# Three small changes to the planner that orders a transformer block's instructions: VectorE may wait a moment, one chain is priced as dependent, one reciprocal goes before a product group

## The chip, the cores and the metric

The kernel runs on one core of one Trainium2 chip. The metric is the device time of one execution in microseconds (us). The engines are TensorE (PE; its weight loads are PEld), VectorE (DVE), ScalarE (ACT), GpSimd (POOL) and SyncE (SP, which issues nearly all DMAs here). They run apart from each other and meet at semaphores. Each executes its own instructions strictly in the order in which the program lists them.

## The reference

One block of a streaming encoder on x of 512 tokens by 1024 channels, float32:

```python
x = x + 0.5 * swiglu_ffn(rms_norm(x), w13, w2)          # first feed-forward half step, 2816 hidden
h = rms_norm(x)
a, g, q, k, v, f = split(h @ w_in)                      # 512 each, f: 8 heads
y_conv = conv_module(a, g)    # a*sigmoid(g), causal depthwise conv of 31 taps, LayerNorm, silu
# forgetting attention, 8 heads of 64, causal:
D = cumsum(log_sigmoid(f + b_f))
y_attn = softmax(q @ k.T / 8 + D[t] - D[s]) @ v
x = x + concat(rms_norm(y_conv), rms_norm(y_attn)) @ w_out
x = x + 0.5 * swiglu_ffn(rms_norm(x), w13b, w2b)        # second half step
out = rms_norm(x)
```

## The kernel before

Channels lie on the 128 partitions, the 512 tokens along the free axis; x is held on chip as eight tiles of 128x512. Weights stream from HBM in units of 128x1024 or so (`raw`). To keep float32's accuracy at the faster matmul format, each weight and each activation is split in two: ScalarE rounds it to a high part (`whi`, `xh`), VectorE subtracts to get the low part (`wlo`, `xl`), and a product is three matmuls: high by high, high by low, low by high. The feed-forward down products (tiles `f1p`, `f2p`) are arranged in seven instead of eight sub-products per block pair, which needs sums and differences of weights on VectorE and GpSimd.

The stages in order of time: first feed-forward part (`f1...`); then, in the middle, the mixer: the gated inputs of four convolution tiles (`pg`, `pa`), values and gate logits (`pv`, `zf`), and for four pairs of heads i the products `pq`, `pk`, the scores `s`, their transposes `pt` and the weighted sum `po`; then the output projection (`wo`); then the second feed-forward part (`f2...`) and the final norm with the stores.

Nearly all matmuls belong to a stream of products whose order is fixed (`ORDER = "c0 c1 c2 v c3 a0 a1 n a2 a3 w0 w1 w2 w3"` in the middle). The convolution's 31 taps are a chain of multiply-adds for each tile: tiles 1 and 3 on VectorE (`conv<-u,par,conv`, accumulated in PSUM), tiles 0 and 2 on ScalarE (multiply, `tap`) and GpSimd (add, `acc<-acc,tap`). `conv_norm` normalises the four tiles when all are done.

The forget gates: `values()` makes `zf` in eight small steps, then the log-sigmoid as one joined chain of 16 VectorE instructions on 128x32 tiles (`e`, `lf`). Joined instructions are one step of the plan and are issued together. `gates()` transposes `lf` (`pc`, behind the product `pq` of the first pair of heads), makes the cumulative sums with one scan (`cum`), writes them to DRAM on SP's queue, from where each head's row is loaded, spread over all partitions (`ck`). The step that adds `ck` to the scores and takes the row minimum is `sm<-s,ck` with `mn`.

The order of every engine's instructions is not written by hand: the block first records all steps in a `Plan`, and `schedule` then puts them in order. Each step has a cost from `price` (a formula per engine and operation) and a rank: the longest path of costs from it to the end, plus its own urgency, a number that the code gives some steps (`URGENT_V`, `URGENT_LF`, `URGENT_LN`, `URGENT_STATS` 200; the attention 80; the `x` updates in the feed-forward part 50; q and k 3; weights' splits and taps none). The scheduler walks through a modelled time: for each engine it picks, among the steps whose inputs all have a place already, the one that can start first, and among equals the one of the highest rank; of the engines' picks the earliest is put in the order. A step that depends on another of the same engine may start 0.03 us behind its end on VectorE (`SAME`), while the engine counts as free 0.08 us before that end (`OVERLAP`). The price of a step that joins several instructions is the sum of theirs.

The end of the kernel: the last down products are made in parts: tokens 0 to 255, then 256 to 383 and 384 to 511. For each part `scales` sums the squares (`ssq_out`), takes the square root on ScalarE and the reciprocal on VectorE (`rc_out`), spreads it by two matmuls (`rb_out`), and `finish` multiplies three groups of tiles by it on VectorE and stores each (`out_d`), from SP's queue, but for one group of the last part from ScalarE's.

All instructions are emitted in one place, so the profile puts them all at line 248; tiles' names tell them apart.

## Time and profile before

| | before |
|---|---|
| median of 3 runs | 943.43 us (942.79 to 943.44) |
| the profiled execution | 943.39 us |
| its span, first to last instruction | 941.7 us |
| mean granted TensorE clock | 0.998 of full speed |
| PE busy | 930.4 us (99%), 5277 matmuls |
| DVE busy | 654.4 us (69%), 990 instructions |
| ACT busy | 431.3 us (46%), 676 instructions |
| POOL busy | 155.1 us (16%), 132 instructions |
| HBM read, written | 88.21 MB, 2.11 MB |

Rows of the timeline give the start in us from the span's start, the length in us, engine, line, operation, output <- inputs, form and count; in brackets the idle time of the engine just before and what ended it. Where several instructions of a kind stand in a row, they are merged and the length is that of all. Rows of waits give the total, the number of times and the longest. Rows by stretches give the stretch, its length and the busy time of PE, PEld, DVE, ACT and POOL with the counts of instructions, then the granted clock, the DMA share and GB/s. The lengths of matmuls overlap, since they are pipelined: they start some 0.227 us apart at 128x512.

### The profile page before, as it was taken

How to read it: one execution, taken by the hardware profiler on the slowest of the kernel's cores; microseconds unless marked ns; L12 is line 12 of the kernel's file. 1: busy time of each engine (PE TensorE's matmuls, PEld its weight loads, DVE VectorE, ACT ScalarE, POOL GpSimd, SP SyncE). 2: the span in 40 equal slices, each digit the busy share in tenths (PEclk: the TensorE clock that was granted, in tenths of full speed). 3: DMA queues.
4: the chain of work that ended last, by engine and by line, in shares of the span. 5: the costliest groups of instructions: out<-in, count | busy, mean ns of one | idle time of the engine just before them, and what ended most of it. 6: DMA issues, size and time to landing. Idle time of an engine off the chain costs nothing.

```text
span 941.7 us, 13473 instructions
## 1 busy us (share of the span) xinstructions
PE 930.4 (99%) x5277; PEld 794.2 (84%) x5277; DVE 654.4 (69%) x990; ACT 431.3 (46%) x676; POOL 155.1 (16%) x132
## 2 busy tenths in 40 slices
PE   9999999999999999999999999999999999999997
PEld 7888999988999888897776777888899988999887
DVE  6655887756876475799987776555777755876554
ACT  6433433334333245666878655333433333433344
POOL 1000211001112000889763000000111001111000
PEclk9999999999999999999999999999999999999999
DMA  7222323132333132223221112223332222332222
GB/s 248 91 90 93 131 90 112 69 109 71 134 113 106 52 97 104 91 93 109 90 69 49 64 68 90 90 90 98 122 116 90 90 90 90 123 101 96 67 84 90
DMA packets 34207, 91.19 MB, mean 97 GB/s; under 512 B 3544, under 2 KB 13912, under 8 KB 34144
## 3 DMA queue, kind: packets, MB, share of 16 engines
q1 hardware_dynamic: 33600, 90.13, 28.3%
q8 instruction: 41, 0.67, 0.3%
q10 hardware_dynamic: 544, 0.20, 0.1%
q14 instruction: 22, 0.18, 0.1%
HBM read 88.21 MB, written 2.11 MB: 96 GB/s over the span
## 4 chain that ended last, share of the span: by engine, by line
PE 92%; DVE 4%; ACT 2%; issue 1%; DMA 1%; SPq 0%; DVEq 0%
PE f2g L248 13%; PE f2u L248 13%; PE f1u L248 13%; PE f1g L248 13%; PE f2p L248 9%; PE f1p L248 9%; PE wo L248 5%; PE f1o L248 3%; PE f2o L248 3%; PE s L248 2%; PE pg L248 2%; PE pa L248 2%; DVE conv L248 2%; PE pq L248 1%; PE pv L248 1%; PE pk L248 1%
## 5 line engine op out<-in xcount | busy, mean ns | idle before, releaser
L248 ACT CAST whi<-raw 128x1024 fp32r<-128x1024 f32 (+3 forms) x152 | 150.8, 992 | 266.1 <-issue 84.5
L248 DVE TENSOR_TENSOR wlo<-raw,whi 128x1024 fp32r<-128x1024 f32 (+3 forms) x152 | 185.6, 1222 | 17.5 <-ACT whi L248 17.0
L248 POOL TENSOR_TENSOR acc<-acc,tap 128x512 f32<-128x512 f32 x60 | 90.9, 1516 | 82.9 <-ACT tap L248 78.4
L248 PE MATMUL f1u<-xh,whi 128*128 128x512 f32 x176 | 68.9, 391 | 0.4 <-ACT xh L248 0.4
L248 PE MATMUL f1u<-xl,whi 128*128 128x512 f32 x176 | 68.6, 390 | 0.3 <-DVE xl L248 0.3
L248 PE MATMUL f2g<-xh,whi 128*128 128x512 f32 x176 | 68.7, 390 | 0.0
L248 PE MATMUL f2g<-xl,whi 128*128 128x512 f32 x176 | 68.6, 390 | 0.0
L248 PE MATMUL f2u<-xh,whi 128*128 128x512 f32 x176 | 68.6, 390 | 0.0
L248 PE MATMUL f1u<-xh,wlo 128*128 128x512 f32 x176 | 68.5, 389 | 0.0
L248 PE MATMUL f2u<-xl,whi 128*128 128x512 f32 x176 | 68.5, 389 | 0.0
L248 PE MATMUL f2u<-xh,wlo 128*128 128x512 f32 x176 | 68.5, 389 | 0.0
L248 PE MATMUL f2g<-xh,wlo 128*128 128x512 f32 x176 | 68.5, 389 | 0.0
L248 PE MATMUL f1g<-xh,whi 128*128 128x512 f32 x168 | 65.8, 392 | 0.0
L248 PE MATMUL f1g<-xl,whi 128*128 128x512 f32 x168 | 65.7, 391 | 0.0
L248 PE MATMUL f1g<-xh,wlo 128*128 128x512 f32 x168 | 65.6, 390 | 0.0
L248 POOL TENSOR_TENSOR f2S<-raw 128x512 f32<-128x512 f32 x8 | 11.3, 1408 | 311.7 <-DMA raw<-w2b 227.8
L248 DVE TENSOR_TENSOR f2un<-f2u,rstd_f2in 128x512 f32<-128x512 f32 x22 | 15.2, 691 | 63.4 <-PE f2u L248 63.4
L248 POOL TENSOR_TENSOR f1S<-raw 128x512 f32<-128x512 f32 x8 | 10.4, 1295 | 261.7 <-DMA raw<-w2a 194.4
L248 DVE TENSOR_TENSOR f1un<-f1u,rstd_in 128x512 f32<-128x512 f32 x22 | 15.2, 690 | 54.5 <-PE f1u L248 54.5
L248 ACT ACTIVATE tap<-u,par 128x512 f32<-128x512 f32 x60 | 42.3, 720 | 16.0 <-POOL acc L248 15.8
L248 DVE SCALAR_TENSOR_TENSOR conv<-u,par,conv 128x512 f32<-128x512 f32 x60 | 45.1, 752 | 1.2
L248 PEld LDWEIGHTS f1u<-xh,whi 128*128 128x128 f32 x176 | 33.2, 188 | 7.8 <-ACT xh L248 0.8
(420 smaller groups left out, 2408.1 us busy)
## 6 DMA issues: line engine op xcount, KB each, us to landing
raw<-w13b SPq DMA_DIRECT2D x44, 512.0 KB, 3.5
raw<-w13a SPq DMA_DIRECT2D x42, 512.0 KB, 3.4
raw<-w2a SPq DMA_DIRECT2D x16, 512.0 KB, 3.6
raw<-w2b SPq DMA_DIRECT2D x16, 512.0 KB, 3.6
raw<-wag SPq DMA_DIRECT2D x8, 512.0 KB, 3.5
raw<-wqk SPq DMA_DIRECT2D x8, 512.0 KB, 3.5
raw<-wo SPq DMA_DIRECT2D x8, 512.0 KB, 3.4
raw<-w2a SPq DMA_DIRECT2D x16, 192.0 KB, 2.4
```

Of the source, the lines that this page charges most:

```text
L248: ins = getattr(target, method)(*real, **kw)
```

## The change

- In `schedule`, once VectorE's pick is known, a loop looks at its other ready steps. One that can start later than the pick, but by less than 0.4 us and 0.6 of the pick's own cost (`AHEAD`), and whose rank is more than 80 above the pick's (`MORE`), takes the pick's place: VectorE then waits for it.
- In `values`, the joined log-sigmoid chain is priced 16 x 0.035 = 0.56 us higher.
- In `scales` of the very last part, the last product of the group before (tokens 256 to 383, tiles 6 and 7), which `finish` has noted in `waiting`, is made dependent on the new reciprocal, so that it cannot be put ahead of it.
- The load of `x` at the start gets a branch for `k < 0` and a condition `k >= 0`; k runs from 0 to 7.

```diff
+AHEAD, MORE = 0.4, 80.0
...
                 pick = None
+                soon = []
                 for op in ready[e]:
...
                     key = (t, -rank, op.index)
+                    soon.append((op, t))
                     if pick is None or key < pick[0]:
                         pick = (key, t, op)
+                if pick and e == "V":
+
+                    until = pick[1] + min(AHEAD, 0.6 * pick[2].cost)
+                    for op, t in soon:
+                        if pick[1] < t < until and op.rank - MORE > -pick[0][1]:
+                            pick = ((t, -op.rank, op.index), t, op)
...
                 V.reciprocal(c, c)
+                if ts.stop == T:
+
+                    waiting[0].before[id(plan.ops[-1])] = plan.ops[-1]
                 r = bank(*banks[1])[:, :n * P]
...
                     V.tensor_mul(xt, xt, r.over(b - a))
+                    waiting[:] = [plan.ops[-1]]
...
-        behind, summed = [], []
+        behind, summed, waiting = [], [], []
...
+        if k < 0:
+            with plan.urgent(7000.0 - 100 * k):
+                S.dma_start(out=xs[k], in_=x_d[:, k, :])
         with plan.urgent(4950.0 - 100 * k):
-            Q.dma_start(out=xs[k], in_=x_d[:, k, :])
+            if k >= 0:
+                Q.dma_start(out=xs[k], in_=x_d[:, k, :])
...
-        plan.join("V")
+        chain = plan.join("V")
+
+        chain.cost += 16 * 0.035
```

## The prediction

> **What bounds the kernel.** I read the page first, then the list of what TensorE waited for, then busy time by stretches, and last the instruction order of single engines round each wait that was left.

> ```profile
> span 941.7 us, 13473 instructions
> PE 930.4 (99%) x5277; PEld 794.2 (84%) x5277; DVE 654.4 (69%) x990; ACT 431.3 (46%) x676; POOL 155.1 (16%) x132
> ```

> ```profile
> PE s L248 <- DVE k L248: 1.5, 1, 1.5
> PE pt L248 <- ACT pT L248: 1.5, 1, 1.5
> PE warm L248 <- POOL eps L248: 1.1, 1, 1.1
> PE rb_out L248 <- DVE rc_out L248: 1.0, 1, 1.0
> PE s L248 <- DVE mn L248: 0.5, 1, 0.5
> ```

> The page says that TensorE is busy 99% of the span. A change that only puts VectorE's instructions (DVE) in another order takes nothing from TensorE's 930.4 us; it can shorten only the 941.7 - 930.4 = 11.3 us in which TensorE stands still. The waits say where these are: one at the start (`warm`, untouched), three in the middle (1.5 for `k`, 1.5 for `pT`, 0.5 for `mn`: 3.5 us), one at the end (`rc_out`); the rest is the last update and store behind the last product.

> ```profile
> 421.00:435.00 14.00, 14.00 (x64) 11.59 (x63) 13.27 (x29) 9.08 (x15) 12.04 (x10) 1.00 0.23 75
> 435.00:450.00 15.00, 13.04 (x64) 10.02 (x63) 14.76 (x25) 8.63 (x16) 12.68 (x7) 1.00 0.40 141
> 511.00:530.00 19.00, 17.50 (x153) 13.62 (x153) 16.22 (x28) 15.80 (x31) 5.67 (x7) 1.00 0.11 40
> 530.00:925.00 395.00, 395.00 (x2201) 339.47 (x2200) 261.58 (x382) 157.73 (x230) 21.76 (x16) 1.00 0.27 93
> ```

> The columns are length, then busy time of PE, PEld, DVE, ACT and POOL. VectorE's mean of 69% hides a stretch where it is the tight engine: 13.27 of 14 us and 14.76 of 15 us from 421 to 450, and it is there that TensorE loses 1.96 us. Behind 530 it has 133 us to spare while TensorE never stops.

> **Part 1: the gates' steps cost 0.56 more in the plan.** No instruction is added; the plan's clock of VectorE moves. The joined chain has 16 instructions. By `price`, those that touch PSUM cost 0.15 + 32 x 0.00105 = 0.18 (six), 0.15 + 32 x 0.00118 = 0.19 (nine `scalar_tensor_tensor`), and the reciprocal 0.35: 3.14 us. On the chip:

> ```profile
> 421.18 0.18 DVE L248 SCALAR_TENSOR_TENSOR e<-zf 128x32 f32<-128x32 f32 x1
> 421.29 1.22 DVE L248 TENSOR_TENSOR wlo<-raw,whi 128x1024 fp32r<-128x1024 f32 x1
> 422.42 0.19 DVE L248 TENSOR_SCALAR e<-e 128x32 f32<-128x32 f32 x1
> 425.96 0.19 DVE L248 SCALAR_TENSOR_TENSOR lf<-e,e 128x32 f32<-128x32 f32 x1
> ```

> From 422.42 to 425.96 + 0.19 = 426.15 are 3.73 us, and 3.14 + 0.56 = 3.70. So the plan believed VectorE to be 0.56 us further on than it was, and now it does not. The chain's own result isn't urgent: `gates` uses `lf` only behind the product of `pq`, at 435. What the correction moves is the choice among the instructions that follow:

> ```profile
> 435.83 0.38 PE L248 MATMUL pc<-ident,lf 128*8 128x128 f32 x2
> 441.28 0.39 PE L248 MATMUL pk<-xh,wlo 128*128 128x512 f32 x1
> 444.54 0.46 PE L248 MATMUL s<-k,q 128*128 128x128 f32 x2 [1.51 <-DVE k L248]
> 436.32 1.55 DVE L248 SCALAR_TENSOR_TENSOR conv<-u,par,conv 128x512 f32<-128x512 f32 x2
> 437.78 0.68 DVE L248 SCALAR_TENSOR_TENSOR q<-pq,rstd_f1n 64x512 f32<-64x512 f32 x1
> 438.38 1.20 DVE L248 TENSOR_TENSOR_SCAN cum<-one,pc 8x512 f32<-8x512 f32 x1
> 441.39 0.69 DVE L248 SCALAR_TENSOR_TENSOR q<-pq,rstd_f1n 64x512 f32<-64x512 f32 x1
> 442.12 1.55 DVE L248 SCALAR_TENSOR_TENSOR conv<-u,par,conv 128x512 f32<-128x512 f32 x2
> 443.70 0.69 DVE L248 TENSOR_TENSOR k<-pk,rstd_f1n 128x512 f32<-128x512 f32 x1
> 444.96 2.06 DVE L248 TENSOR_TENSOR wlo<-raw,whi 128x1024 fp32r<-128x1024 f32 x1
> ```

> The product `pk` ends at 441.28 + 0.39 = 441.67, yet `k` starts at 443.70, behind two convolution taps that were issued when `k` could already run: the wait of 1.51 us. In the plan a tap may start only 0.03 behind the tap before it and another instruction 0.08 before that tap's end, so a ready `k` always wins over a tap. Two taps ahead of it mean that in the plan `k` came ready only after the second tap was due. A plan that is 0.56 later here sees it ready one tap sooner, unless the overhang was more than 0.56 of a tap's pitch of 1.55 / 2 = 0.78, which leaves some 0.56 / 0.78, 7 in 10 by my estimate. **Term: -0.78 us**, `k` one tap earlier. Bounds: -1.51 (both taps go) and +1.29, if instead the `wlo` that now stands behind `k` comes ahead of it in the place of one tap (2.06 + 0.78 - 1.55, an estimate from these rows). I take the middle reading because it needs no other instruction to change place. Late next, behind `k`, is that `wlo`, and behind it `mn`, whose wait of 0.5 us I leave as it is.

> [...]

> **Part 2: VectorE waits for far more urgent work.** In `schedule` the new loop looks at instructions that are in `ready`, whose inputs all have a place in the order already, so it can wait only for a result that is being made, and at most 0.4 us. A rank is the longest path to the end plus the step's own urgency. The attention's steps (urgency 80) are not 80 above a tap of the last convolution tile: the tap's own path, through the rest of its taps, the normalisation and the first half of the output product, is longer. `k` and `q` have urgency 3. So it can touch the eight `zf` steps and the scan (urgency 200), the sums of squares (200), and in the two feed-forward parts splits against the updates of `x`, which are due a whole group of columns later. Behind 530 the row above gives the cover: 133 us of VectorE against waits of 0.4. Between 396 and 440 it costs at most 9 x 0.4 = 3.6 us of VectorE, and what queues behind are the taps. They have a cover too:

> ```profile
> 477.10 0.75 DVE L248 SCALAR_TENSOR_TENSOR conv<-u,par,conv 128x512 f32<-128x512 f32 x1
> 481.38 3.34 POOL L248 TENSOR_TENSOR acc<-acc,tap 128x512 f32<-128x512 f32 x2 [0.97 <-ACT tap L248]
> ```

> The normalisation needs all four tiles, and GpSimd's ends at 484.72, 6.9 us behind VectorE's last tap at 477.85. Without that cover 3.6 us would go straight onto the normalisation and from there to `wo`. If the scan passes `q`, the cumulative sums leave up to 0.60 us earlier (438.38 - 437.78), their DMA to DRAM and the two loads of `ck` on SP's queue with them, ahead of no weight load that TensorE waits for; `q` is 1.2 later and still long before `k`. **Term: 0**, bounds -0.5 (the wait for `mn` goes) and +0.8 (a tap's pitch lost ahead of `k`).

> **Part 3: the last reciprocal ahead of a product group.**

> ```profile
> 935.54 0.26 ACT L248 ACTIVATE rc_out<-ssq_out,eps 128x1 f32<-128x1 f32 x1
> 935.85 0.41 DVE L248 TENSOR_TENSOR x<-x,rb_out 128x256 f32<-128x256 f32 x1
> 936.19 0.15 DVE L248 RECIPROCAL rc_out<-rc_out 128x1 f32<-128x1 f32 x1
> 936.49 0.46 PE L248 MATMUL rb_out<-ident,rc_out 128*128 128x128 f32 x2 [0.98 <-DVE rc_out L248]
> 936.98 1.35 DVE L248 TENSOR_TENSOR x<-x,rb_out 128x256 f32<-128x256 f32 x3 [0.64 <-PE rb_out L248]
> 936.51 0.47 SPq L248 DMA_DIRECT2D out_d<-x  x1
> 937.43 0.37 SPq L248 DMA_DIRECT2D out_d<-x  x1
> ```

> The square root ends at 935.80, the third product of the group before stands from 935.85, and the reciprocal starts at 936.19. With the new order it starts where that product started, about 935.86: 0.33 us earlier, and the chain broadcast, last products, last store follows without another partner. The passed product then runs from about 935.97 to 936.38, inside the wait for the broadcast (936.98 - 0.33 = 936.65). Its store moves from 936.51 to some 936.6 and occupies SP's queue until 937.07; the next one is due at 937.43 - 0.33 = 937.10: just free. **Term: -0.33**, bounds 0 and -0.41 (the whole product).

> The moved `x` loads add nothing: `k < 0` never holds in a loop from 0, and the other condition always does.

> **Sum.** -0.78 + 0 - 0.33 = -1.11 us. The profiled execution took 943.39 us (span 941.7), the median of the runs is 943.43, which is the same. 943.39 - 1.11 = 942.3 us.

> **The rivals.**
> - *Only the tail moves.* `k` keeps its two taps, as the plan's error at this point may be larger than 0.56: the plan put `q`, whose product ends before the transposes `pc` at 435.83, at 437.78. Time 943.39 - 0.33 = 943.1. The scan's late place speaks for it; that 0.56 is most of a tap speaks against.
> - *Faster: the middle waits close.* With `k` at once and `mn` no longer late it is 1.51 + 0.5 + 0.33 = 2.34 us: 941.1. The `pT` wait is ScalarE's:

> ```profile
> 507.43 1.52 ACT L248 ACTIVATE acc<-acc,par 128x512 f32<-128x512 f32 x2
> 511.50 1.32 ACT L248 ACTIVATE yh<-acc,par 128x512 fp32r<-128x512 f32 x2
> 512.73 0.45 ACT L248 COPY pT<-pt 128x384 f32<-128x384 f32 x1
> ```

>   The copy stands behind the whole row of normalisation steps from 507.43; if the shifted plan puts it some steps forward, 1.5 more goes, 939.6 in all. It needs luck, since no part aims at it.
> - *Slower: a doubled split ahead of `k`.* One mechanism: the later plan finds a weight's split due before `k`, and on the chip it collides with GpSimd:

> ```profile
> 433.25 2.31 DVE L248 TENSOR_TENSOR wlo<-raw,whi 128x1024 fp32r<-128x1024 f32 x1
> 432.66 5.42 POOL L248 TENSOR_TENSOR acc<-acc,tap 128x512 f32<-128x512 f32 x3
> ```

>   This split took 2.31 us beside the accumulations, against 1.22 for the same one at 421.29. Put ahead of `k` with both taps still there it gives 943.39 - 0.33 + 2.31 = 945.4. It decides from 2.2 us of new wait on. For it: the stretch is full, and the `wlo` at 444.96 stands right behind `k`. Against: it would have to jump only one place, yet keep both taps ahead. [...]
> - *Small loss inside the noise band:* the waits of part 2 are spent in vain and a tap's pitch reaches TensorE once or twice: 943.39 - 0.33 + 0.78 to + 1.56, 943.8 to 944.6.

> **How the numbers follow.** Forecast 0.36 (its own range 941.5 to 943.0), only the tail 0.20, small loss 0.08, faster 0.22, slower 0.14. 0.2% is 1.89 us, about what a measurement of this kernel can tell from no change: below 941.5 is faster, above 945.3 slower. So faster 0.22, same 0.36 + 0.20 + 0.08 = 0.64, slower 0.14. The range runs from 940.6, half of the faster case's second step, to 945.3, where the slower case begins; about 0.05 lies below it and 0.14 above.

> **What would show it.** In the profile after: TensorE's busy time within 1 us of 930.4; the wait of `s` for `k` near 0.7 instead of 1.5, with one tap between the second `q` and `k`; the last reciprocal right behind the square root and ahead of a product of 128x256, the wait for `rc_out` near 0.65; no wait of TensorE beyond 530 before the tail. Wrong I would be if a wait for `wlo` or a second wait for `pT` appears between 421 and 530, or if the waits there vanish altogether: the plan is greedy, and a small shift of its clock can change any choice behind 422.

## The result: slower by 2.8 us, and the profile after

| | before | after |
|---|---|---|
| median | 943.22 us (7 runs, 942.57 to 943.59) | 946.02 us (7 runs, 944.72 to 947.26) |
| ratio, with its 95% interval | | 1.003 (1.002 to 1.004) |
| the profiled execution, its span | 943.39, 941.7 us | 946.79, 945.0 us |
| mean granted TensorE clock in it | 0.998 | 0.996 |

The forecast was 942.3 us in a range of 940.6 to 945.3. The changed kernel lies above it. All its instructions stand at line 249 instead of 248. The page's first lines, then what TensorE waited for (total, times, longest, in us):

```profile
span 945.0 us, 13474 instructions
PE 933.1 (99%) x5277; PEld 795.6 (84%) x5277; DVE 656.9 (70%) x990; ACT 432.6 (46%) x677; POOL 153.9 (16%) x132
```

```profile
PE pa L249 <- DVE wlo L249: 2.8, 1, 2.8
PE warm L249 <- POOL eps L249: 1.1, 1, 1.1
PE rb_out L249 <- DVE rc_out L249: 0.7, 1, 0.7
PE wo L249 <- DVE yl L249: 0.6, 1, 0.6
PE f1p L249 <- DVE x L249: 0.5, 1, 0.5
PE f2p L249 <- DVE x L249: 0.4, 1, 0.4
```

Two things changed at once. TensorE is busy 2.7 us longer with the same 5277 matmuls. And the waits for `k` (1.5), `pT` (1.5) and `mn` (0.5) are gone, but a single one of 2.8 us for a weight's split stands where before there was none, in the last convolution tile's product `pa`; behind it come 0.6 for `yl` and, in the two feed-forward parts, 0.5 and 0.4 for updates of `x`. VectorE's timeline round the new wait (start, length):

```profile
421.66 0.19 DVE L249 SCALAR_TENSOR_TENSOR e<-zf 128x32 f32<-128x32 f32 x1
421.76 0.75 DVE L249 SCALAR_TENSOR_TENSOR conv<-u,par,conv 128x512 f32<-128x512 f32 x1
422.42 0.19 DVE L249 TENSOR_SCALAR e<-e 128x32 f32<-128x32 f32 x1
...
425.96 0.19 DVE L249 SCALAR_TENSOR_TENSOR lf<-e,e 128x32 f32<-128x32 f32 x1
426.07 2.24 DVE L249 TENSOR_TENSOR wlo<-raw,whi 128x1024 fp32r<-128x1024 f32 x1
428.23 0.68 DVE L249 TENSOR_TENSOR gn<-pg,rstd_f1n 128x512 f32<-128x512 f32 x1
```

Before, the same split stood at 421.29, ahead of the log-sigmoid chain, and took 1.22 us. Now the chain (422.42 to 426.15, 3.73 us as before) stands ahead of it, and the split runs beside GpSimd's accumulations and takes 2.24. In the traces of before and after a split of 128x1024 that begins while GpSimd runs no TENSOR_TENSOR takes 1.19 to 1.23 us. One that begins beside a running one takes longer by about the time that is left of it, but for one (at 439.51 before, 1.19 us beside an accumulation of 3.69); an accumulation that begins beside a running split is longer too. So here: before, the split began first, and the accumulation that began at 421.87 took 1.78 us instead of 1.3; after, an accumulation runs from 425.96 to 427.23, 1.16 us beyond the split's start, and the split takes 1.02 us more. The split ends at 428.31; TensorE had been ready since 425.56:

```profile
425.17 0.39 PE L249 MATMUL pa<-xl,whi 128*128 128x512 f32 x1
428.37 0.50 PE L249 MATMUL pa<-xh,wlo 128*128 128x512 f32 x1 [2.81 <-DVE wlo L249]
428.70 0.39 PE L249 MATMUL pa<-xh,whi 128*128 128x512 f32 x1
...
430.46 0.63 PE L249 MATMUL pa<-xh,whi 128*128 128x512 f32 x1
430.89 0.63 PE L249 MATMUL pa<-xl,whi 128*128 128x512 f32 x1
...
435.10 0.39 PE L249 MATMUL pq<-xh,whi 128*128 128x512 f32 x1
```

The wait isn't all. From 429.6 on the same matmuls start 0.43 us apart instead of 0.227, until 433. The 22 matmuls left of `pa` take 435.10 - 428.37 = 6.73 us, where 22 x 0.227 are 4.99: 1.74 us more, and that is most of TensorE's longer busy time. By stretches (length, busy time of PE, PEld, DVE, ACT, POOL, then the granted clock) the clock is seen to be halved:

```profile
425.00:428.00 3.00, 0.56 (x3) 0.13 (x1) 2.83 (x7) 1.93 (x3) 2.84 (x3) 1.00 0.00 0
429.00:430.00 1.00, 1.00 (x5) 0.81 (x4) 1.00 (x2) 1.00 (x2) 0.46 (x1) 0.82 0.71 143
430.00:433.00 3.00, 3.00 (x8) 2.32 (x7) 2.89 (x5) 1.52 (x3) 2.66 (x2) 0.50 0.72 243
433.00:434.00 1.00, 1.00 (x6) 0.80 (x5) 0.96 (x2) 0.00 (x0) 0.21 (x1) 0.97 0.44 176
435.00:450.00 15.00, 15.00 (x73) 12.22 (x72) 14.14 (x18) 9.24 (x13) 12.35 (x9) 1.00 0.31 107
```

With the first matmul of some tiles as marks, the span's 3.4 us more come from here:

| from the first matmul of | to that of | before | after | difference |
|---|---|---|---|---|
| start | `f1p` | 106.8 | 106.3 | -0.5 |
| `f1p` | `pg` (tile 0) | 254.9 | 255.6 | +0.8 |
| `pg` | `pq` (pair 0) | 68.4 | 73.2 | +4.7 |
| `pq` | `wo` | 80.0 | 77.4 | -2.5 |
| `wo` | `f2g` | 66.3 | 66.8 | +0.5 |
| `f2g` | first `rb_out` | 351.8 | 352.4 | +0.6 |
| first `rb_out` | end | 13.4 | 13.3 | -0.2 |

The first row differs from execution to execution (105.9 to 108.0 in the 13 profiles of this study). The stages behind it hardly do: where two kernels have the same order in a stage, the clock is the same and no update of `x` is passed over, its length agrees within 0.04 us, with two exceptions (0.34 and 0.14). So the marks show differences that the medians can't. The 0.8 and the 0.6 are the stages with the waits for updates of `x`.

The 4.7 are, but for 0.2, the wait of 2.8 and the slow clock of 1.74. The -2.5 behind it are the old waits for `k`, `mn` and most of that for `pT`: with TensorE 4.7 us later, VectorE and ScalarE are no longer late there. That is why the row 435 to 450 now shows TensorE busy for all of its 15.00 us.

**Why the plan did this.** In the changed plan's own clock, VectorE's pick at 418.02 us was the split (rank 452). The joined log-sigmoid chain, rank 593, could start 0.07 us later. That is inside the 0.4 us and more than 80 above, so VectorE waited 0.07 us and took up a step of 3.70 us. The rule looks at how soon the urgent step can start, not at how long it runs, nor at when the passed step is due.

### The profile page after: what moved, and what is told of

Read it like the earlier page. It is cut to its first block, busy times and chain, and to the rows that moved or that the text cites. A ratio compares the mean times of both kernels' runs of the same rounds, so it can differ in the third digit from the quotient of the medians.

```text
span 945.0 us, 13474 instructions
## 1 busy us (share of the span) xinstructions
PE 933.1 (99%) x5277; PEld 795.6 (84%) x5277; DVE 656.9 (70%) x990; ACT 432.6 (46%) x677; POOL 153.9 (16%) x132
## 4 chain that ended last, share of the span: by engine, by line
PE 91%; DVE 4%; ACT 2%; DMA 1%; issue 1%; SPq 0%; DVEq 0%; ACTq 0%
PE f2g L249 13%; PE f2u L249 13%; PE f1u L249 13%; PE f1g L249 13%; PE f2p L249 8%; PE f1p L249 8%; PE wo L249 4%; PE f1o L249 3%; PE f2o L249 3%; PE pa L249 2%; PE pq L249 2%; PE s L249 2%; PE pk L249 2%; PE pg L249 2%; PE pv L249 1%; DVE conv L249 1%
## 5 line engine op out<-in xcount | busy, mean ns | idle before, releaser
L249 POOL TENSOR_TENSOR acc<-acc,tap 128x512 f32<-128x512 f32 x60 | 88.1, 1468 | 86.9 <-ACT tap L249 82.4
L249 PEld LDWEIGHTS f1u<-xl,whi 128*128 128x128 f32 x176 | 33.0, 188 | 7.9 <-DVE xl L249 1.1
```

The source lines that it names most:

```text
L249: ins = getattr(target, method)(*real, **kw)
```

## Experiments

Each was run in turn with the kernel before; the medians of before in the three groups of runs (a, b, c) are 943.35, 943.37 and 943.36 us. Changes in order were made behind the plan where one place was meant, so that everything else stays as it was.

**One split back ahead of the chain.** The changed kernel's order, with only that one instruction moved:

```diff
         order = self.schedule()
+        order.remove(self.split)                          # wlo of tile 3's pa
+        order.insert(order.index(self.chain), self.split) # ahead of the log-sigmoid
...
```

> The order of the changed kernel with one instruction moved: the split wlo for the product pa of convolution tile 3 is issued in front of the log-sigmoid chain instead of behind it. All else stays in the changed kernel's order. Theory 1 (this one place is the loss): TensorE's wait for wlo of 2.8 us goes, and with it the 1.7 us that the slow clock behind it cost (22 matmuls in 6.73 us instead of 22 x 0.227 = 4.99), so about 946.8 - 4.5 = 942.2 us in the profiled execution, 0.1% below the kernel before. Theory 2 (the reordering as a whole costs, many small delays): at most half of it goes, 944.5 us or more. Under theory 1 the clock stays at 1.00 from 421 to 440.

Measured 944.52 us (943.73 to 945.38, 11 runs), ratio 1.0014 (1.0005 to 1.0023). The wait of `pa` is gone and the clock is 1.00 throughout 421 to 435; in its place some of the old waits come back:

```profile
PE s L249 <- DVE k L249: 1.3, 1, 1.3
PE rb_out L249 <- DVE rc_out L249: 0.7, 1, 0.7
PE wo L249 <- DVE yl L249: 0.6, 1, 0.6
PE pk L249 <- DVE wlo L249: 0.6, 1, 0.6
PE f1p L249 <- DVE x L249: 0.4, 1, 0.4
```

One instruction's place carries 1.5 of the 2.8 us. The other 1.2 or so remain. So theory 1 was right in its signs (no wait, full clock) and wrong in its time, since it counted none of the waits that come back.

**The same split moved behind the chain in the kernel before.**

```diff
         order = self.schedule()
+        order.remove(self.split)
+        order.insert(order.index(self.chain) + 1, self.split)
...
```

> The mirror image: the order of the kernel before with the same one split moved from in front of the log-sigmoid chain to right behind it, nothing else. Theory 1: TensorE waits for this split at pa, some 1.5 us (chain from 421.9 to 425.5, split to 426.7, needed at 425.2) up to 2.6 us if GpSimd doubles it; VectorE's total work is unchanged, so the later wait for k (1.5 us) shrinks by about as much, and the time is 943.2 to 944.9 us, the upper end if the clock falls behind the wait. Theory 2: the place of the split is harmless, 943.2 us with no wait for wlo.

Measured 945.0 us (944.37 to 945.46), ratio 1.0016 (1.0007 to 1.0025): this single move costs 1.65 us. The chain starts earlier here than in the changed kernel (421.29, not 422.42) and the split takes 1.48 us, not 2.24 (GpSimd's accumulation ends 0.40 us behind its start), so the wait is shorter:

```profile
PE pa L248 <- DVE wlo L248: 1.7, 1, 1.7
PE pt L248 <- ACT pT L248: 1.5, 1, 1.5
PE s L248 <- DVE k L248: 1.1, 1, 1.1
```

The granted clock stays at 1.00 behind this wait of 1.7.

**The reciprocal alone** (the changed kernel with rule and price switched off, so that only the dependence in `scales` is left beside the kernel before; one pair of VectorE's instructions changes places).

```diff
...
+                if ts.stop == T:
+                    waiting[0].before[id(plan.ops[-1])] = plan.ops[-1]
```

> The kernel before with the reciprocal's edge alone: on every engine the order differs from the kernel before by one swap, the last reciprocal ahead of one product. Prediction: 0.33 us less, the wait for rc_out 0.65 instead of 1.0. Rival: something else ends last (the stores), 0.0.

Measured 943.24 us, ratio 0.9997 (0.9988 to 1.0006). The wait for `rc_out` is 0.7 instead of 1.0, and from the first `rb_out` the last one comes 0.33 us earlier (7.93 us instead of 8.26). The end comes only 0.16 us earlier (13.27 instead of 13.44), because the last store takes longer from issue to landing: 2.30 us instead of 2.15. In the 13 profiles this goes with its distance to the store two ahead of it: 2.30 to 2.34 where that is 1.06 to 1.09 us (eight profiles), 2.13 to 2.17 where it is 1.37 to 1.40 (five). In the median what the step is worth is less than these runs can tell from nothing.

**Without the rule** (the chain's price and the reciprocal stay).

```diff
-                if pick and e == "V":
+                if False and pick and e == "V":
```

> The changed kernel without the waiting rule: the dearer chain and the reciprocal's edge remain. The prediction's mechanism by itself: k behind one tap instead of two, wait for k 0.7 us, 942.3 us. Rival: the shifted plan makes another wait in the mixer and the time is 943.0 us or more; if it is about 946, the chain's price and not the rule is to blame.

Measured 943.62 us (942.59 to 944.72), ratio 1.0002 (0.9993 to 1.001). The profiled execution took 942.64 (span 940.9). Its waits:

```profile
PE wo L249 <- DVE yl L249: 1.0, 1, 1.0
PE rb_out L249 <- DVE rc_out L249: 0.7, 1, 0.7
PE wo L249 <- ACT yh L249: 0.6, 1, 0.6
PE s L249 <- DVE k L249: 0.6, 1, 0.6
```

The rule's whole loss is gone. The price did what the forecast said, one tap instead of two between the second `q` and `k`, a wait of 0.6 where 0.7 was forecast, and the wait for `mn` is gone too. But in place of the 1.5 us for `pT` stand 1.6 us at `wo` for the normalised convolution outputs, and in the median the gain isn't seen. In the profile it is: from `pq` to `f2g` this kernel takes 0.65 us less than before (145.58 instead of 146.23), and with the tail's 0.17 it is 0.83 us shorter from `f1p` to the end. Its three runs at a mean clock of 0.998 took 942.64 to 942.81 us, its four at 0.996 943.55 to 944.01, and the four at 0.997 942.59 to 944.72.

A second finding comes from the plan alone: with the rule on, the chain's price changes nothing. The changed kernel without the 0.56 has the same order on all five engines.

**The wait filled with idle matmuls.** The changed kernel, with 11 more matmuls inside the 2.8 us, overwritten by the product itself:

```diff
...
+            if k == 0:
+                for m in range(fill):          # 11 for pa of tile 3, else 0
+                    PE.matmul(ps, hi[:, k], ah[k], start=True, stop=True)
+                step.cost = 0.0
```

> The changed kernel with eleven idle matmuls (11 x 0.227 = 2.5 us) in front of the first matmul of the product pa that waits for the late split. Each starts its sum anew, so they leave nothing in the result. They fit into the wait of 2.8 us: if that wait alone costs, nothing changes (946.0 us) and the wait shows as 0.3 us behind the idle matmuls. Theory A (TensorE's standstill brings the slow clock, which costs up to 1.7 us more): with TensorE kept busy the clock stays at 1.00 behind it, the median falls by 0.8 to 1.7 us to 944.3 to 945.2, and the spread of the runs (2.5 us before) narrows to about 1 us. Theory B (the slow clock has another cause, the loads that run at that time or chance): clock near 0.5 for some us as before, 946 us.

Measured 946.16 us (944.85 to 948.11, 6 runs), ratio 1.0029 (1.0017 to 1.0041). In the profile the clock is 1.00 from 425 to 435 and `pg` to `pq` takes 71.6 us instead of 73.2, which is the 1.6 us of slow clock; but the median didn't fall. This profile has waits elsewhere that the other lacks or has smaller, `xh` at the start 1.1 and `f2p` 1.0: by the marks the start took 0.9 us longer, the stage with `f2p` 0.6 and the tail 0.1, so that the span is the same 945.0. So the run settled the clock in one profile and not the time.

**The split ahead, and no update of `x` passed over.** The rule also lets VectorE leave updates of `x` in the feed-forward parts; here it may not, and the split is moved as in the first experiment:

```diff
-                if pick and e == "V":
+                if pick and e == "V" and pick[2].urgent != URGENT_X:
...
```

> The changed order with the split in front of the chain (as in the first run of this study) and with the waiting rule not applied where VectorE's pick is an update of x in the feed-forward parts. TensorE's, ScalarE's, GpSimd's and SP's orders are the same as there; only VectorE's order in the two feed-forward parts returns to that of the kernel before. If the rule costs there, the waits of f1p and f2p for x (0.4 and 0.2 us) go and the time falls from 944.5 to 943.9 us. Rival: these waits are covered by later slack, 944.5 us as before.

Measured 943.66 us (943.05 to 944.36), ratio 1.0003 (0.9994 to 1.0012). The waits of `f1p` and `f2p` are gone, and 0.86 us against the first experiment with them. With both harms of the rule out, what is left is no difference from before that can be measured.

**`k` first, in the kernel before.** The two taps ahead of `k` are put behind it:

```diff
+        at = order.index(self.k0)
+        taps = [o for o in order[:at] if o.engine == "V"][-2:]
...
+        order[at + 1:at + 1] = taps
...
```

> The kernel before with the two convolution taps that stand ahead of k put behind it, nothing else. The prediction's reading of that wait (k is late by its taps, and TensorE gains what k gains) gives 1.5 us less, 941.8 us, with no wait of s for k. Rival, formed after the run without the rule: what is late next takes the gain. s runs 1.5 us earlier, but the scores' next step needs ck from DRAM and stands behind the 2.06 us split, so the wait for mn grows from 0.5 to about 2 us and the time stays at 943.3 us.

Measured 944.44 us (942.86 to 945.25), ratio 1.0006 (0.9997 to 1.0015). The wait for `k` is gone, and what was late next takes the gain: the wait for `mn` is 2.0 us, where before it was 0.5.

```profile
PE s L248 <- DVE mn L248: 2.0, 1, 2.0
PE pt L248 <- ACT pT L248: 1.5, 1, 1.5
```

Its runs fall in two groups: five at a mean granted clock of 0.998 took 942.86 to 943.81, and six at 0.996 or 0.997 took 944.44 to 945.25. The kernel before has no run at 0.996 in 88.

**A rule for short steps only**, that passes over no update of `x`; price and reciprocal as in the changed kernel:

```diff
-                if pick and e == "V":
+                if pick and e == "V" and pick[2].urgent != URGENT_X:
...
-                        if pick[1] < t < until and op.rank - MORE > -pick[0][1]:
+                        if pick[1] < t < until and op.cost < 2.0 and op.rank - MORE > -pick[0][1]:
```

> The changed kernel with the rule limited: VectorE may wait only for steps that cost under 2 us (so not for the log-sigmoid chain), and not in the place of an update of x. The plan is made anew, so the mixer's order differs in many places. If the two harms named are all, it is no slower than the run without the rule: 943.6 us or less, no wait for wlo and none of f1p or f2p. Rival: any new order of the mixer brings waits of its own, 944 to 945 us.

Measured 942.39 us (941.98 to 943.58, 11 runs), ratio 0.999 (0.9981 to 0.9998): the best of all kernels here, 1.0 us below before and 3.6 below the changed one. Price and reciprocal are in it too. By the marks it is 0.92 us shorter than before from `f1p` to the end, where the kernel without the rule is 0.83 shorter: by the two profiles, both at a mean clock of 0.998, the rule for short steps adds 0.1 us. The medians of the two are 1.2 us apart; no run here has a mean clock of 0.996, and four there have, but that this is all of it isn't shown.

**The long wait left in, without and with filling.** The last question was what the wait and the clock are worth apart. First the changed kernel with no update of `x` passed over, the split left behind the chain:

> The changed kernel, with the rule kept from passing over updates of x; the order of VectorE differs in 28 rows, the split of `wlo` stays behind the log-sigmoid chain. Theory A (the two harms add, and the wait of 2.8 us for `wlo` also slows TensorE's clock for some 3.5 us in part of the runs): wait of `pa` for `wlo` 2.8, waits of `f1p` and `f2p` for x gone, 946.0 - 0.9 = 945.1, runs spread over some 2 us with a lower mean clock (0.996) in the longer ones. Theory B (the clock has nothing to do with the spread): same median, runs within 1 us of each other.

Measured 945.54 us (943.62 to 947.64, 11 runs), ratio 1.0021 (1.0012 to 1.003). Three of its runs have a mean clock of 0.998 (943.62 to 945.12), the other eight 0.995 to 0.997 (945.2 to 947.64). The profiled execution, the longest, shows the slow clock twice as long as in the changed kernel:

```profile
427.00:428.00 1.00, 0.00 (x0) 0.00 (x0) 1.00 (x1) 0.81 (x1) 0.92 (x2) 0.98 0.00 0
428.00:429.00 1.00, 0.40 (x1) 0.40 (x2) 1.00 (x2) 0.00 (x0) 1.00 (x1) 0.50 0.00 0
430.00:433.00 3.00, 3.00 (x8) 2.32 (x7) 2.93 (x4) 1.76 (x3) 2.42 (x2) 0.50 0.72 235
434.00:435.00 1.00, 1.00 (x5) 0.77 (x3) 0.76 (x1) 0.00 (x0) 0.11 (x1) 0.61 0.00 0
435.00:440.00 5.00, 5.00 (x23) 4.13 (x22) 3.08 (x4) 2.77 (x4) 3.30 (x3) 1.00 0.00 0
```

Then the same with the 11 matmuls of the filling; no other row of any engine differs:

> As the kernel without the passed updates of x, with 11 matmuls more ahead of the waiting product of `pa`, which are overwritten by the product itself, so that TensorE isn't idle in the wait. Theory A: no run at a mean clock of 0.996, no slow stretch behind the wait, and a median some 0.7 us lower than without the filling (1.7 us in the share of runs that had the slow clock, about 4 in 10). Theory B: the same median within 0.3 us.

Measured 944.22 us (943.59 to 944.77, 11 runs), ratio 1.0009 (1.0 to 1.0017). TensorE does 2.5 us more work, and the kernel is 1.3 us faster; its runs spread over 1.2 us instead of 4.0, and none is below a mean clock of 0.997.

```profile
421.00:435.00 14.00, 13.66 (x61) 10.99 (x59) 13.21 (x31) 8.63 (x14) 9.77 (x9) 1.00 0.25 89
```

Every one of its runs is faster than nine of the eleven without the filling. That is the theory that the idle wait slows the clock, shown in the time and not only in one profile. The same test on the kernel with `k` first, 8 matmuls into the wait for `mn`:

```diff
...
+            if k == 3:
+                for m in range(fill):          # 8 for pq of pair 1, else 0
+                    PE.matmul(ps, hi[:, k], ah[k], start=False, stop=False)
+                step.cost = 0.0
```

> The kernel before with the two taps put behind `k`, as measured already (944.44, its runs in two groups, 943.1 and 944.6), and 8 matmuls more ahead of the wait of 2.0 us for `mn`. They repeat a block of the product `pq` of the second pair of heads into the same sum, which alters q of that pair. Theory A (the idle 2.0 us slow the clock in about half of the runs): wait for `mn` near 0.2, the group at a mean clock of 0.996 gone, median 943.1 to 943.4. Theory B: the two groups stay, median 944.4.

Measured 943.73 us (943.01 to 944.72, 11 runs), ratio 1.0005 (0.9996 to 1.0014). The wait is 0.24, the runs at 0.996 are gone and the median is 0.7 lower, but it isn't the 943.1 to 943.4 of the theory, and runs at a clock of 0.998 or 0.999 reach 944.7. So the clock is part of that kernel's spread and not all of it.

**The 2.8 us put together**, from the medians: not passing over `x` takes 0.5 (946.02 to 945.54), no slow clock 1.3 (to 944.22), the split back in its place 0.6 (to 943.66). That is 2.4 of 2.8. Taken in the other order, the split's place was 1.5 and `x` 0.86. The 95% interval of each ratio is some 0.8 us to either side, so of the three only the 1.3, where the runs hardly overlap, is clear by itself.

The marks part them better. From `f1p` to the end the profiled execution of the changed kernel is 3.9 us longer than that of before (838.74 and 834.81):

- Updates of `x`: 1.4, from `f1p` to `pg` 0.76 and from `f2g` to the first `rb_out` 0.61. In the four kernels whose rule spares `x` neither is there (0.01 us at most); in the two others that pass over them both together are 1.1 and 1.9.
- The slow clock: 1.6. From `pg` to `pq` it takes 73.16, with the wait filled 71.57.
- The wait itself: 0.7. With the wait filled `pg` to `pq` is still 3.13 longer than with the split in its place (68.44), but `pq` to `wo` is 2.39 shorter (77.45 and 79.84), since the old waits are covered.
- The rest of the order and the reciprocal: 0.2, which is what the kernel with both harms out has left.

## Why the prediction was wrong, step by step

**Part 2 failed: "what queues behind are the taps", and with it "Term: 0", bounds -0.5 and +0.8.** Measured, the rule costs 2.4 us (946.02 with it, 943.62 without). Three things in it were wrong.

- *What stands behind the waiting instruction.* Not only taps: the splits of the weight stream are ready all the time and rank below the gates' steps as well. A tap had a cover (the normalisation is GpSimd's); a split is due when TensorE reaches it, and this one was due 2.7 us behind its old end (421.29 + 1.22 = 422.51), as a row of before shows that the prediction doesn't use:

```profile
425.18 0.39 PE L248 MATMUL pa<-xh,wlo 128*128 128x512 f32 x1
```

- *Which steps it can wait for.* The list named the `zf` steps and the scan, and left out the joined chain between them, which has the urgency of the logits too. Part 1 had already measured its 3.73 us.
- *The price of a wait.* It was counted as 0.4 us at most for each. What the passed step loses is the wait and the whole step that goes ahead: 0.07 + 3.70 in the plan. From the rows of before this could have been worked out: put behind a chain that starts in its place, the split starts at 421.29 + 3.73 = 425.02 and ends at 426.2, or at 427.3 if it takes the 2.31 us of the one at 433.25, against a due time of 425.18: 1.0 to 2.1 us of wait. The kernel before with only that move measured 1.7, with the split at 1.48 us.

The rival of a doubled split had the right mechanism in the wrong place: it looked for it ahead of `k`, where the wait had been, and not at a product that had no wait. This one split took 2.24 us beside GpSimd's accumulation, against 1.22 where it began first. That a wait for `wlo` would show the forecast wrong had been said; that it would slow the matmuls behind it had not.

**The cover "133 us of VectorE against waits of 0.4" behind 530 failed in the same way**, at a smaller size. Spare time on the whole doesn't help a single update of `x` that TensorE waits for: 0.5 and 0.4 us at `f1p` and `f2p`, 1.4 us of the profiled execution by the marks (0.5 to 0.9 by the medians).

**Part 1 was right in its mechanism where it acts, and its term was had there, but not in the changed kernel.** Without the rule, `k` comes one tap sooner (a wait of 0.6 for 0.7 forecast), and from `pq` to `f2g` the profile is 0.65 us shorter, where -0.78 was forecast. That the two are so near is partly luck: the waits for `k`, `mn` and `pT` are 2.9 us shorter together and those at `wo` 1.6 us longer, and of all this the sum had only `k`. In the median the gain isn't there; four runs have a mean clock of 0.996, but some at 0.997 are as slow, so what takes it stays open. In the changed kernel the price has no effect at all, and the wait for `k` is gone for another reason, because TensorE is late itself. Nor is a sooner `k` a gain by itself: with `k` first in the kernel before, `mn` takes all of it. "Late next" had been named (the split, then `mn`), but left at its old 0.5.

**Part 3 was right in its steps, and its term is half.** The wait for `rc_out` is 0.65 where "near 0.65" was forecast, with the reciprocal ahead of the 128x256 product. But the end comes 0.16 us earlier and not 0.33: "without another partner" was wrong, since the last stores stand closer together and the last one lands 2.30 us behind its issue instead of 2.15.

```profile
939.38 0.16 DVE L249 RECIPROCAL rc_out<-rc_out 128x1 f32<-128x1 f32 x1
939.46 0.40 DVE L249 TENSOR_TENSOR x<-x,rb_out 128x256 f32<-128x256 f32 x1
939.68 0.46 PE L249 MATMUL rb_out<-ident,rc_out 128*128 128x128 f32 x2 [0.65 <-DVE rc_out L249]
```

**"TensorE's busy time within 1 us of 930.4" was wrong:** 933.1. The sum was made on the ground that VectorE's order takes nothing from TensorE's busy time. It added to it here, by the clock: 1.74 of the 2.7 us.

## What to carry to other kernels

A rule that lets an engine wait a little for an urgent step must be priced by the length of the step that it lets ahead, and against the due time of what it passes over; limited to short steps, the same rule did no harm, and the kernel with it was 1.0 us faster than before. When a change reorders an engine, look first for the steps that have no wait today and see how much room each has; the next loss comes there and not where the waits already are. Read a change of 1 us by the marks of stages as well as by the medians: here most stages repeat within 0.04 us, and the runs only within 1 to 2. Look at the clock behind a long TensorE wait too: after the waits of 2.81 us here it fell to half for 3.41 and 6.83 us, and by the marks the first of these cost 1.6 us, the wait itself 0.7. Filling the wait with matmuls that do nothing took 1.3 us off the median of one kernel (945.54 to 944.22) and nothing off that of the other (946.02 and 946.16).

## What the runs showed of the hardware that was not expected

```profile
428.60 0.80 PE L249 MATMUL pa<-xh,wlo 128*128 128x512 f32 x1 [2.81 <-DVE wlo L249]
...
436.62 0.39 PE L249 MATMUL pq<-xh,whi 128*128 128x512 f32 x1
```

How much of a step was idle can be read from the profiles. The step ahead of each slow stretch held 2.14 us (425.56 to 428.37 from 426.23 on) and 2.17 us (425.79 to 428.60 up to 427.96) of idle TensorE. In the kernel before with the split moved the whole wait of 1.70 us lay in one step (424.65 to 428.06), and the clock stayed. With `k` first the 2.04 us (445.63 to 447.67) were parted at 446.02, 1.65 of them in one step, and the clock stayed. So in these four profiles the half clock came behind steps with 2.14 and 2.17 us of idle TensorE, and not behind those with 1.65 and 1.70. That some runs have it and others don't because the steps happen to lie otherwise against the wait is the author's estimate from these numbers, as only one run of each kernel has a trace.

The mean clocks of the runs without a trace agree only in part. In every profile the clock also falls at the end, 2.6 to 5.7 us ahead of the last instruction, and that alone gives means of 0.997 to 0.999. A mean that rounds to 0.996 takes at least 6.6 us at half clock (2 x 0.0035 x 942), so it points to a slow stretch elsewhere. Such runs came with 2.8 us in one wait (3 of 7 and 5 of 11), with 2.0 (5 of 11), and without the rule (4 of 11). With a longest wait of 1.7 us, or the wait filled, there was none, and none in 88 runs of the kernel before, whose waits of 1.51 and 0.45 us lie too far apart for one step. The four without the rule stay open: the profile of that kernel has waits of 0.61 and 1.01 us at `wo`, 1.62 us that one step could hold, which is less than the 1.70 that did not slow the clock. Open are also the spread of the first filled kernel up to 948.11 us, and the spread that is left in the kernel with `k` first and filled.
